# Attention and SwiGLU on one core: the second chunk's preparation moved among the first chunk's products, the down weights' sums stored ahead in DRAM, gated blocks in halves

## The chip, the cores and the metric

One core of one Trainium2 chip (trn2). The metric is the device time of one execution, in microseconds. The kernel before took 1845.11 us (median of three runs, 1843.49 to 1845.51).

## The reference

One layer on two token groups, 1024 and 512 tokens of width 1024, all in float32:

```python
y = neighbourhood_attention(rms_norm(x, norm_mix), na_w_qkv, na_rpb, na_w_o)
x = x + y
x = x + swiglu(rms_norm(x, norm_ffn), ffn_w_gate, ffn_w_up, ffn_w_down)
return rms_norm(x, norm_final)

def swiglu(x, w_gate, w_up, w_down):          # (1024 x 2816), (1024 x 2816), (2816 x 1024)
    return (silu(x @ w_gate) * (x @ w_up)) @ w_down
```

The attention is over windows of 8 rows and 16 columns of a grid 64 wide, 16 heads. The change touches what comes behind it.

## The kernel before

Every float32 operand of a product is split into a high and a low part (`split`, L138 a cast on ScalarE, L139 a subtraction on VectorE), and every product runs in three passes (high by high, high by low, low by high).

The stages follow each other: norm and V projection (to 157 us), attention with its q and k projections (to about 760), the o-projection (L586, its last matmul ends at 803.1), then the feed-forward part and the final norm. x1, the input plus the attention, is kept in DRAM (`x1_d`).

The feed-forward part works on two chunks of 768 tokens. All its big products use a scheme of seven products for a 2x2 block product, with operands that are sums and differences of the four blocks:

- `norm2` and `pair` (L661 to L687) load two x1 tiles, take root and gain (`rms`, L115 to L122), transpose them (L668), and `operands` makes the seven operands: for chunk 0 they are split into `hops` in SBUF, for chunk 1 they are stored to `hop_d` in DRAM. Both happen before the first product of chunk 0, interleaved with the o-projection of the last tiles.
- `unit(c, p, hops)`, 11 for each chunk, does 7 gate and 7 up products (`blocks`, `product`), each of 12 matmuls of 128x384 (L754). The weights come in raw tiles of 512 KB (`w_raw`, L714), `w_ops` makes sums (`wt`) and splits (`wa`, `ws`). ScalarE copies the banks into `c` tiles and applies Silu, VectorE adds and multiplies, and GpSimd makes four sums of gated blocks (`gs`, L800 to L803) and stores seven blocks to `gop_d` (L805).
- Between the chunks the operands of chunk 1 are read back from `hop_d` (L815) and split.
- Down: seven products n, each over 6 token tiles and 11 blocks i; `d_op` loads weight blocks (`dr`, L834) and for four of the seven makes differences on GpSimd (L848 to L857, `tk`), `g_op` loads a whole gated block (`gr`, 128x1408, L864) and splits it into `go`. 33 matmuls of 128x512 (L910) fill a bank. The results are added up in `u2`, `u4` and the `c` tiles, and `finish` (L884 to L893) applies the final norm.

The program is written in this order, and the framework's list scheduler orders the instructions of each engine by its own estimate of their times; on the chip each engine, and each of the three DMA queues (SP's, ScalarE's, GpSimd's), then takes its rows strictly in that order. Buffers come from pools; a pool opened after another is closed takes its space.

## Time and profile before

| | us |
|---|---|
| median of 3 runs | 1845.11 (1843.49 to 1845.51) |
| the profiled execution | 1845.18 |
| its span, first to last instruction | 1843.4 |
| TensorE busy | 1754.1 (95%) |
| VectorE / ScalarE / GpSimd busy | 1192.9 / 863.7 / 448.4 |
| mean granted TensorE clock | 0.985 |
| chunk 0's first product starts | 810.10 |
| chunk 1's first product ends its wait | 1172.54 |
| last up product ends, first down matmul | 1481.6, 1498.72 |
| last addition behind the last down matmul | 1835.16 |

PE is TensorE's matmul, PEld its weight load, DVE VectorE, ACT ScalarE, POOL GpSimd, SP the engine whose queue issues most DMAs; SPq, ACTq and POOLq are the queues. A group's row reads: line, engine, operation, written tile <- read tiles, shape, count | busy us, mean ns of one | idle time before them and what ended it. A row of the timeline reads: start us, length us, then the same, and in brackets the wait before it and what ended it.

### The profile page before, as it was taken

What the parts mean: (1) busy time and instruction counts of PE and PEld (TensorE: products, weight loads), DVE (VectorE), ACT (ScalarE), POOL (GpSimd) and SP (SyncE); (2) the same over time, 40 slices, a digit from 0 to 9 for tenths busy, and PEclk for the clock granted to TensorE, in tenths of its full rate; (3) what the DMA queues carried; (4) which work ended last, traced back from release to release, by engine and by line L of the source; (5) the groups of instructions that cost most, each with busy time, mean ns of one, the idle gap of its engine ahead of it and who ended that gap; (6) DMA issues with size and microseconds to landing.
All of it is one profiled execution on the core that took longest, in us unless ns stands there. A gap on an engine that the chain in (4) does not pass through costs nothing.

```text
span 1843.4 us, 25648 instructions
## 1 busy us (share of the span) xinstructions
PE 1754.1 (95%) x9178; PEld 1522.5 (83%) x9178; DVE 1192.9 (65%) x2191; ACT 863.7 (47%) x1706; POOL 448.4 (24%) x495
## 2 busy tenths in 40 slices
PE   8999999999999999979999999999999969999898
PEld 6877777777767777868999999899999958887676
DVE  4401877777896566768777777867777444545654
ACT  4411776766785554544443444444443333333322
POOL 1211000000130000112243342424243323526420
PEclk9999999999999999988999999999999979999999
DMA  7755334333464443676343434544333277635732
GB/s 245 221 183 160 111 105 113 108 101 103 126 208 146 133 149 100 221 247 185 108 121 118 133 110 151 164 129 125 108 120 107 68 272 245 225 130 191 232 129 100
DMA packets 222048, 278.80 MB, mean 151 GB/s; under 512 B 25600, under 2 KB 171776, under 8 KB 221920
## 3 DMA queue, kind: packets, MB, share of 16 engines
q1 hardware_dynamic: 201824, 210.69, 37.3%
q0 software_dynamic: 18368, 60.18, 9.5%
q10 hardware_dynamic: 1728, 6.29, 1.1%
q8 instruction: 72, 1.18, 0.3%
q14 instruction: 56, 0.46, 0.1%
HBM read 213.20 MB, written 76.43 MB: 157 GB/s over the span
## 4 chain that ended last, share of the span: by engine, by line
PE 68%; DVE 10%; DMA 9%; ACT 5%; issue 3%; SPq 2%; POOL 2%; DVEq 0%; ACTq 0%; POOLq 0%
PE pa L754 20%; PE pd L910 12%; PE pd L754 10%; PE pgv L278 7%; PE pg L332 6%; PE pb L754 5%; DMA vr<-v_d 5%; PE pgo L586 3%; DMA dr<-ffn_w_down 2%; PE pss L394 2%; PE ptt L420 2%; DVE pT L424 2%; SPq L378 2%; PE po L431 2%; ACT s L405 1%
## 5 line engine op out<-in xcount | busy, mean ns | idle before, releaser
L910 PE MATMUL pd<-wd,go 128*128 128x512 f32 x1386 | 323.0, 395 | 30.5 <-ACT go L138 20.4
L910 PEld LDWEIGHTS pd<-wd,go 128*128 128x128 f32 x1386 | 263.0, 191 | 90.4 <-ACT go L138 21.6
L754 PE MATMUL pa<-h,ws 128*128 128x384 f32 x1056 | 201.8, 339 | 2.9 <-ACT c L777 2.1
L754 PE MATMUL pa<-h,wa 128*128 128x384 f32 x1056 | 195.1, 338 | 7.0 <-ACT wa L138 4.5
L754 PE MATMUL pd<-h,ws 128*128 128x384 f32 x1056 | 198.3, 335 | 1.2 <-ACT h L138 0.6
L332 PE MATMUL pg<-hTp,whl 128*128 128x512 f32 x768 | 193.7, 399 | 0.0
L754 PEld LDWEIGHTS pa<-h,wa 128*128 128x128 f32 x1056 | 185.8, 190 | 8.9 <-ACT wa L138 5.2
L139 DVE TENSOR_TENSOR ws<-wt,ws 128x1024 fp32r<-128x1024 f32 x88 | 108.6, 1235 | 127.1 <-ACT ws L138 126.7
L754 PEld LDWEIGHTS pa<-h,ws 128*128 128x128 f32 x1056 | 185.1, 189 | 6.7 <-ACT c L777 4.3
L754 PEld LDWEIGHTS pd<-h,ws 128*128 128x128 f32 x1056 | 184.5, 188 | 1.8 <-ACT h L138 1.0
L332 PEld LDWEIGHTS pg<-hTp,whl 128*128 128x128 f32 x768 | 139.9, 188 | 27.5 <-issue 0.4
L805 POOL DMA_DIRECT2D gop_d<-c x66 | 50.5, 765 | 387.4 <-DVE c L796 380.3
L405 ACT ACTIVATE s<-s,mx 128x384 f32<-128x384 f32 (+1 forms) x192 | 110.7, 580 | 67.3 <-DVE mx L402 67.1
L586 PE MATMUL pgo<-wo,oh 128*128 128x512 f32 x576 | 139.3, 392 | 0.2 <-DVE oh L139 0.2
L139 DVE TENSOR_TENSOR wa<-wr,wa 128x512 fp32r<-128x512 f32 x132 | 117.8, 897 | 18.4 <-ACT wa L138 17.8
L138 ACT CAST ws<-wt 128x1024 fp32r<-128x1024 f32 x88 | 92.6, 1053 | 68.6 <-PE pd L754 65.4
L586 PEld LDWEIGHTS pgo<-wo,oh 128*128 128x128 f32 x576 | 105.6, 188 | 20.7 <-DVE oh L139 0.6
L138 ACT CAST go<-gr 128x1408 fp32r<-128x1408 f32 x42 | 57.7, 1374 | 131.2 <-PE pd L910 114.0
L138 ACT CAST wa<-wr 128x512 fp32r<-128x512 f32 x132 | 81.4, 621 | 62.8 <-PE pb L754 40.0
L754 PE MATMUL pb<-h,wa 128*128 128x384 f32 x528 | 102.0, 340 | 3.4 <-DVE c L774 3.4
L332 PE MATMUL pg<-hTs,whl 128*128 128x512 f32 x384 | 102.6, 404 | 0.8 <-DVE q L343 0.8
L424 DVE TENSOR_TENSOR pT<-ptt,pT 128x384 fp32r<-128x384 f32 (+1 forms) x192 | 90.0, 507 | 17.3 <-ACT pT L423 16.5
(138 smaller groups left out, 2859.6 us busy)
## 6 DMA issues: line engine op xcount, KB each, us to landing
gr<-gop_d SPq DMA_DIRECT2D x42, 704.0 KB
dr<-ffn_w_down SPq DMA_DIRECT2D x99, 256.0 KB
wr<-ffn_w_gate SPq DMA_DIRECT2D x44, 512.0 KB
wr<-ffn_w_up SPq DMA_DIRECT2D x44, 512.0 KB
wr<-na_w_qkv SPq DMA_DIRECT2D x38, 512.0 KB
gop_d<-gs POOLq DMA_DIRECT2D x88, 192.0 KB, 4.4
gop_d<-c POOLq DMA_DIRECT2D x66, 192.0 KB, 2.8
vr<-v_d SPq DMA_DIRECT2D x192, 64.0 KB
```

The source lines that it names most:

```text
L138: nc.scalar.copy(hi, raw)
L139: nc.vector.tensor_tensor(lo, raw, f32(hi), ALU.subtract)
L278: nc.tensor.matmul(pg, hh[a][:, k, c:c + P], wv[k // 2][b][:, k % 2], start=(k == 0 and i == 0), stop=(k == KB - 1 and i == 2))
L332: nc.tensor.matmul(pg, w[:, a, k, :], h[b][:, k, c:c + 512], start=(k == 0 and i == 0), stop=(k == KB - 1 and i == 2))
L378: nc.sync.dma_start(out=raw[:, j * P:(j + 1) * P], in_=src[:, BS[j]:BS[j] + 32, :])
L394: nc.tensor.matmul(pt[:, :n], q[h * HD:(h + 1) * HD, a, j].rearrange("p r i -> p (r i)"), kv[:, krow:krow + nrow, BS[j]:BS[j] + 32], start ...
L405: nc.scalar.activation(s[:, :n], s[:, :n], AF.Exp, bias=mx, scale=-1.0, accum_out=sm)
L424: nc.vector.tensor_tensor(pT[:, :n, 1], pv, f32(pT[:, :n, 0]), ALU.subtract)
L586: nc.tensor.matmul(pg, ohs[k // 4][:, a, k % 4], wo[:, b, k, n * 512:(n + 1) * 512], start=(k == 0 and i == 0), stop=(k == KB - 1 and i == 2))
L754: nc.tensor.matmul(bank[:, :HT], a(y, k), b[:, z, k], start=start and k == 0 and i == 0, stop=k == KB // 2 - 1 and i == 2, skip_group_chec ...
L805: nc.gpsimd.dma_start(out=gop_d[i, 3 * c:3 * c + 3, :, p].rearrange("j q t -> q j t"), in_=a.rearrange("q (j t) -> q j t", j=3))
L910: nc.tensor.matmul(pd, go[:, y, i], wds[i][:, z], start=(i == 0 and m == 0), stop=(i == NP - 1 and m == 2))
```

## The change

Four things, in the order in which they run.

1. The preparation of chunk 1 (`pair1`) becomes a generator, stepped by a `tick` behind each product of units 1, 2 and 3 of chunk 0. It uses four tiles t0 to t3 that exist once each. The gain is applied behind the transposes on VectorE, from a column form `gT` that is loaded at the very start; the root is applied by `nc.scalar.mul`; the operands' differences are made on GpSimd. For chunk 0 `pair0` does the same ahead of the products as before.
2. At the changes (the last unit of chunk 0, the first and last of chunk 1) the up products are interleaved with the gate products at a lag of three, and the operands of chunk 1 are read back (`reload`) one by one behind the last up products of unit (0, 10), through t0 to t3.
3. In chunk 1 `down_sums` makes the differences of down weights that `d_op` made in the down stage, on GpSimd, in 11 iterations, and stores them to DRAM (`wt_d`). It uses t0, t1 and t2.
4. The down stage loads half gated blocks (6 and 5 of the 11) and stored sums, with buffers placed one by one in the space that the last units leave. x1 tiles and half of the results go through GpSimd's queue. The squares and, for the second half of the rows, one multiplication by the final gain are done earlier.

To make room, the weight tiles `wa`, `ws` and `wt` have 2 buffers each (6, 3 and 3 before), with a second pool of 2 for the last `wa` of a block.

```diff
+        gT = cpool.tile([P, KB], F32, name="gT")
+        nc.sync.dma_start(out=gT, in_=g_ffn.rearrange("(k p) -> p k", p=P))
...
+        def pair1(j):
+            xs = []
+            for n, t in enumerate((CT + j, CT + 3 + j)):
+                xn = temp(2 * n)
+                xt = temp(2 * n + 1).rearrange("p (k t) -> p k t", k=KB)
+                yield from norm2(t, xn, xt)
+                xs.append(xt)
+            tt = [temp(2 * n).rearrange("p (s k t) -> p s k t", s=2, k=KB // 2) for n in range(2)]
+
+            def dst(i, op):
+                nc.sync.dma_start(out=hop_d[i, :, :, j * P:(j + 1) * P], in_=op)
+            yield from operands(dst, *xs, [tt[n // 2][:, n % 2] for n in range(4)], nc.gpsimd)
+
+        def down_sums():
+
+            for i in range(NP):
+                x, y, z = temp(0), temp(1), temp(2)
+                nc.sync.dma_start(out=x, in_=w_d[2 * i * P:(2 * i + 1) * P, :])
+                nc.sync.dma_start(out=y, in_=w_d[(2 * i + 1) * P:(2 * i + 2) * P, :])
+                yield
+                b11, b12, b21, b22 = x[:, :512], x[:, 512:], y[:, :512], y[:, 512:]
+                t1, t3 = z[:, :512], z[:, 512:]
+                nc.gpsimd.tensor_tensor(t1, b12, b11, ALU.subtract)
+                yield
+                nc.gpsimd.tensor_tensor(t3, b22, b12, ALU.subtract)
+                nc.gpsimd.dma_start(out=wt_d[0][i * P:(i + 1) * P, :], in_=z)
+                yield
+                nc.gpsimd.tensor_tensor(b11, b22, t1, ALU.subtract)
+                yield
+                nc.gpsimd.tensor_tensor(b12, b21, b11, ALU.subtract)
+                nc.gpsimd.dma_start(out=wt_d[1][i * P:(i + 1) * P, :], in_=x)
+                yield
...
+            order = [0] * 7 + [1] * 7
+            if after:
+                order = [0] * LAG + [x for _ in range(7 - LAG) for x in (1, 0)] + [1] * LAG
...
+        prep = (x for j in range(3) for x in pair1(j))
+        tick = ticks(prep, 1)
+        for p in range(NP - 1):
+            unit(0, p, hops, tick if p else idle)
+            if p == NP - 2:
+                reload(0)
+        unit(0, NP - 1, hops, idle, lambda n: reload(n) if n < 7 else None)
+        sums = down_sums()
+        tick = ticks(sums, 2)
+        for p in range(NP):
+            unit(1, p, hops2, tick if p else idle, None if 0 < p < NP - 1 else lambda n: None)
+        for _ in sums:
+            pass
...
+        SRC = {0: (w_d, 0, 0), 1: (w_d, 1, 0), 2: (w_d, 1, 1), 4: (wt_d[0], None, 0), 6: (wt_d[0], None, 1),
+               5: (wt_d[1], None, 0), 3: (wt_d[1], None, 1)}
...
+        for q in range(84):
+            m, tt, h = q // 12, q % 12 // 2, q % 2
+            n = SEQ[m]
+            g_load(q + 3)
+            g_split(q + 2)
+            if q % 12 < NP:
+                d_load(m + 1, q % 12)
+            if q % 12:
+                d_split(m + 1, q % 12 - 1)
```

Where the instructions stand is set by the scheduler. Three places follow; in the rows, a number behind a tile's name is that of one buffer's use, and the brackets hold the semaphores that a row waits for.

SP's queue in chunk 1, around the raw weights of unit 5. Before (wr_13603 and wr_13605 are the two raw tiles of unit 5's up weights):

```order
L714 DMA wr_13339<-ffn_w_up 128x4x256 [waits DMAHW6_49,DVE_49]
L714 DMA wr_13477<-ffn_w_gate 128x4x256 [waits DMAHW7_49,DVE_49]
L714 DMA wr_13479<-ffn_w_gate 128x4x256 [waits DMAHW0_49,DVE_49]
L714 DMA wr_13603<-ffn_w_up 128x4x256 [waits DMAHW1_49,DVE_49]
L714 DMA wr_13605<-ffn_w_up 128x4x256 [waits DMAHW2_49,DVE_49]
L714 DMA wr_13743<-ffn_w_gate 128x4x256 [waits DMAHW3_49,DVE_49]
```

After (wr_13691 and wr_13693 are those two; t0 and t1 are the loads of the weights' sums, t0_14485 that of the eleventh iteration):

```order
L748 DMA t0_14070<-ffn_w_down 128x1024 [waits DMAHW2_49,DMASW5_49]
L749 DMA t1_14294<-ffn_w_down 128x1024 [waits DMAHW7_49,DMAHW3_49,Pool_49]
L769 DMA wr_13559<-ffn_w_gate 128x4x256 [waits DVE_49]
L748 DMA t0_14293<-ffn_w_down 128x1024 [waits DMAHW6_49,DMAHW1_49,DMASW7_49]
L769 DMA wr_13691<-ffn_w_up 128x4x256 [waits DVE_49]
L749 DMA t1_14486<-ffn_w_down 128x1024 [waits DMAHW7_49,Pool_49]
L748 DMA t0_14485<-ffn_w_down 128x1024 [waits DMAHW4_49,DMAHW1_49,DMASW2_49]
L769 DMA wr_13693<-ffn_w_up 128x4x256 [waits DMAHW5_49,DVE_49]
```

Between the raw weights now stand loads of t0, each with a wait for a DMA of GpSimd's queue (DMASW), and all eleven iterations' loads stand ahead of wr_13693.

GpSimd in chunk 1, around the sums and stores of one unit's gated blocks. Before:

```order
L805 DMA gop_d_81<-c_12760 128x3x128 [waits DMASW0_49,DVE_49]
L800 TENSOR_TENSOR gs_12930<-c_12746,c_12760 128x384 [waits DVE_49]
L801 TENSOR_TENSOR gs_12931<-gs_12930,c_12719 128x384 [waits Pool_49]
L802 TENSOR_TENSOR gs_12932<-c_12719,c_12746 128x384
L803 TENSOR_TENSOR gs_12933<-c_12803,gs_12931 128x384 [waits DVE_49,Pool_49]
L805 DMA gop_d_81<-c_12803 128x3x128 [waits DMASW1_49]
L805 DMA gop_d_81<-gs_12933 128x3x128 [waits DMASW2_49,Pool_49]
L805 DMA gop_d_81<-gs_12930 128x3x128 [waits DMASW3_49]
```

After (t2_12888 and t0_12886 belong to the third iteration of the weights' sums, gs_12415 to gs_12418 to unit (1, 0)):

```order
L753 TENSOR_TENSOR t2_12888<-t0_12886 128x512 [waits DMAHW7_49,DMASW4_49]
L755 TENSOR_TENSOR t2_12888<-t1_12887,t0_12886 128x512 [waits DMAHW5_49]
L758 TENSOR_TENSOR t0_12886<-t1_12887,t2_12888 128x512 [waits DMASW5_49,Pool_49]
L876 TENSOR_TENSOR gs_12415<-c_12231,c_12287 128x384 [waits DVE_49]
L756 DMA wt_d0_81<-t2_12888 128x1024 [waits DMASW7_49,Pool_49]
L877 TENSOR_TENSOR gs_12416<-gs_12415,c_12204 128x384 [waits Pool_49]
L878 TENSOR_TENSOR gs_12417<-c_12204,c_12231 128x384
L879 TENSOR_TENSOR gs_12418<-c_12371,gs_12416 128x384 [waits DVE_49,Pool_49]
L881 DMA gop_d_83<-c_12371 128x3x128 [waits DMASW0_49]
L881 DMA gop_d_83<-gs_12418 128x3x128 [waits Pool_49]
L881 DMA gop_d_83<-gs_12415 128x3x128
L881 DMA gop_d_83<-gs_12416 128x3x128 [waits DMASW3_49]
```

The unit's gated sums, which stood alone, now stand inside an iteration of the weights' sums, between its third and its fourth subtraction.

ScalarE in chunk 0, at the first gate products of a unit: of unit 2 after, of one of the first units before. Before:

```order
L792 ACTIVATE c_9464<-c_9464 128x384 [waits DVE_49]
L777 COPY c_9491<-pa_9449 128x384 [waits PE_49]
L780 COPY c_9505<-pd_9451 128x384 [waits PE_49]
L138 CAST ws_9569<-wt_9566 128x1024 [waits Activation_49]
L792 ACTIVATE c_9505<-c_9505 128x384 [waits DVE_49]
```

After (t1 and t3 take the squares of two x1 tiles, L675 scales them; c_9633 and c_9669 are the unit's first two copies of pa):

```order
L669 ACTIVATE t1_9636,ms_9651<-t0_9635 128x1024 [waits DMAHW3_49]
L669 ACTIVATE t3_9725,ms_9744<-t2_9724 128x1024 [waits DMAHW7_49,DMAHW4_49,DVE_49]
L827 COPY c_9633<-pa_9618 128x384 [waits PE_49]
L141 CAST wa_9754<-wr_9750 128x512 [waits Activation_49]
L141 CAST wa_9772<-wr_9752 128x512
L141 CAST wa_9757<-wr_9752 128x512 [waits PE_49,Activation_49]
L675 ACTIVATE t0_9635<-t0_9635,rs_9655 128x1024 [waits Activation_49,Pool_49]
L866 ACTIVATE c_9633<-c_9633 128x384 [waits DVE_49]
L675 ACTIVATE t2_9724<-t2_9724,rs_9748 128x1024 [waits Activation_49,Pool_49]
L834 COPY c_9669<-pa_9618 128x384 [waits PE_49]
L838 COPY c_9684<-pd_9620 128x384 [waits DMASW5_49,PE_49]
```

The Squares and scalings of chunk 1's tiles now stand between the copies and casts of the unit, where only these stood.

389 lines of the change are left out of this document (233 added, 156 removed).

## The prediction

> **What bounds the kernel now.** I read the share of each engine first, then the stage windows, then the places where TensorE stands still. The columns of the windows are: stretch, length, busy time and count of TensorE, weight load, VectorE, ScalarE and GpSimd, granted clock, DMA share, GB/s.
>
> ```profile
> PE 1754.1 (95%) x9178; PEld 1522.5 (83%) x9178; DVE 1192.9 (65%) x2191; ACT 863.7 (47%) x1706; POOL 448.4 (24%) x495
> PEclk9999999999999999988999999999999979999999
> ...
> 806.00:816.00 10.00, 3.34 (x9) 2.60 (x9) 5.03 (x9) 3.16 (x6) 0.87 (x1) 0.63 1.03 342
> 847.00:1150.00 303.00, 303.00 (x1733) 300.98 (x1732) 225.68 (x296) 129.50 (x214) 106.46 (x111) 1.00 0.41 124
> 1150.00:1180.00 30.00, 25.56 (x142) 24.09 (x141) 27.05 (x35) 17.50 (x27) 10.02 (x10) 1.00 0.64 210
> 1180.00:1475.00 295.00, 295.00 (x1697) 293.64 (x1696) 205.20 (x270) 118.38 (x195) 105.72 (x111) 1.00 0.36 109
> 1475.00:1502.00 27.00, 9.45 (x45) 8.12 (x44) 12.78 (x18) 9.88 (x14) 8.41 (x10) 0.67 0.71 248
> ```
>
> TensorE bounds it. Inside the two chunks of up and gate products it never stops (303.00 of 303, 295.00 of 295), while GpSimd has two thirds of its time free. What is to be had lies at three seams: the start of chunk 0, the change of chunk, the start of down. Inside down there is one more:
>
> ```profile
> 803.10 1.04 PE L668 MATMUL pt<-ident,xn 128*128 128x128 f32 x8
> 810.10 3.34 PE L754 MATMUL pa<-h,wa 128*128 128x384 f32 x9 [4.53 <-ACT wa L138]
> 1152.28 4.17 PE pa L754 x24
> 1163.34 7.30 DMA hr<-hop_d
> 1479.36 2.24 PE L754 MATMUL pa<-h,wa 128*128 128x384 f32 x12
> 1498.72 1.22 PE L910 MATMUL pd<-wd,go 128*128 128x512 f32 x2 [17.12 <-ACT go L138]
> 1510.00:1590.00 80.00, 80.00 (x355) 66.24 (x354) 1.00 0.77 266
> 1690.00:1765.00 75.00, 62.83 (x255) 48.87 (x254) 0.95 0.68 223
> 1835.16 0.69 DVE L896 TENSOR_TENSOR u<-u,pd 128x512 f32<-128x512 f32 x1 [3.03 <-PE pd L910]
> ```
>
> A product of 12 matmuls takes 4.17 / 2 = 2.085 us, a unit of 14 products 29.2. The o-projection ends at 803.1, the last up product at 1481.6: 678.5 us against 22 × 29.2 + 48 transposes at 1.04 / 8 = 648.6. So 29.9 are lost, 30 − 25.56 = 4.4 of them at the change of chunk and 25.5 at the start. Down takes 1835.1 − 1481.6 = 353.5; its 1386 matmuls at 80.00 / 355 = 0.2254 need 312.4. Lost: 41.1, of which 17.1 before its first matmul, 12.2 idle in 1690 to 1765, the rest at a lower clock around these (0.67 in 1475 to 1502).
>
> **The change, part by part.** The sum is made against the profiled run's 1845.2 (1843.4 of span and 1.8 around it), 0.1 above the median.
>
> *Load of gT first on SP's queue.* 1024 elements of 4 bytes ahead of the first x tile. No row has its like; a whole 512 KB load is the nearest:
>
> ```profile
> 1010.60 4.64 SPq L714 DMA_DIRECT2D wr<-ffn_w_gate  x2
> ...
> 1013.50:1014.00 0.50, 0.50 (x4) 0.50 (x4) 0.50 (x1) 0.00 (x0) 0.50 (x1) 1.00 0.47 164
> 1014.00:1014.50 0.50, 0.50 (x5) 0.50 (x4) 0.50 (x1) 0.00 (x0) 0.50 (x2) 1.00 0.02 8
> ```
>
> Issued at 1010.6, its bytes are through by about 1014.1: 3.5. The price of gT lies between nothing and that; I take +1.5, nearer to nothing, since it moves 4 KB.
>
> *Start of chunk 0.*
>
> ```profile
> L138 ACT CAST wa<-wr 128x512 fp32r<-128x512 f32 x132 | 81.4, 621 | 62.8 <-PE pb L754 40.0
> L139 DVE TENSOR_TENSOR ws<-wt,ws 128x1024 fp32r<-128x1024 f32 x88 | 108.6, 1235 | 127.1 <-ACT ws L138 126.7
> L138 ACT CAST ws<-wt 128x1024 fp32r<-128x1024 f32 x88 | 92.6, 1053 | 68.6 <-PE pd L754 65.4
> L741 DVE TENSOR_TENSOR wt<-wr x17: 683/684/686, 902.6 to 1136.6; 128x512 f32<-128x512 f32 x17
> ```
>
> The last chunk-1 preparation (hop stores, six loads, splits) leaves it. The first raw tile and its cast now stand ahead of the o-projection's end, so the first product follows at once. The second raw tile lies where wo lay and is loaded from 803.1 on: 3.5 to land and a cast of 0.62, so the second product starts at about 807.3. For the third, ws needs VectorE's two sums (0.7 each, beside subtractions of wa), a Square of 1.06 ahead of it on ScalarE, a cast of 1.05 and a subtraction of 1.24: about 812. Some 4 to 5 are lost, and 2 to 3 to the lower clock (0.63 there before): 7 (5 to 12) instead of 25.5, −18.5.
>
> *Units 2 and 3 of chunk 0.* The scaling of x1 (L675) needs the root from GpSimd, which stands behind the gated sums of the unit before. Behind the scaling, on ScalarE, stands the copy of pa for which the fifth product waits.
>
> ```profile
> 888.90 4.32 PE L754 MATMUL pa<-h,wa 128*128 128x384 f32 x24
> 892.02 1.00 POOL L800 TENSOR_TENSOR gs<-c 128x384 f32<-128x384 f32 x1 [1.81 <-DVE c L796]
> ...
> 898.01 3.06 POOL L805 DMA_DIRECT2D gop_d<-gs  x4
> L119 POOL TENSOR_TENSOR rs<-me,mhalf 128x1 f32<-128x1 f32 x24 | 14.3, 597 | 75.5 <-DVE me L117 75.4
> L115 ACT ACTIVATE xt<-xn 128x1024 f32<-128x1024 f32 x12 | 12.7, 1060 | 14.7 <-DMA xn<-x_d 6.5 <-issue 2.4 <-DVE h L139 2.4
> 1015.33 0.53 ACT L792 ACTIVATE c<-c 128x384 f32<-128x384 f32 x1 [2.39 <-DVE c L774]
> 1015.77 0.46 ACT L777 COPY c<-pa 128x384 f32<-128x384 f32 x1
> ```
>
> A unit begins at 891.0 (the second product from 888.90); GpSimd is free at 901.1, 10.1 later. Two roots of 0.60, two scalings like the Square's 1.06, a Silu and the copy, half a microsecond each: 14.4 after the unit's start, where the fifth product is due at 4 × 2.085 = 8.3. Waiting 6.1, twice: +12 (7 to 15, since the reload of t0 can be later too; less if the order lets the root go first).
>
> *Change of chunk.* The lagged products give the reload three units' room: 4.4 to about 2, −2.4.
>
> *The weights' sums in chunk 1.* Per iteration: load of t0, four subtractions of 128x512 on GpSimd, store of t0. There is one t0, so the next load waits until the store has landed, and these loads stand on SP's queue ahead of the weights: the one of the eleventh iteration ahead of the second raw tile of unit 5's up weights. Whatever the serial cycle costs, the weights wait for it.
>
> ```profile
> L802 POOL TENSOR_TENSOR gs<-c 128x384 f32<-128x384 f32 x22 | 31.6, 1437 | 0.0
> L848 POOL TENSOR_TENSOR tk<-dr,tk 128x512 f32<-128x512 f32 x11 | 19.7, 1811 | 12.4 <-DMA dr<-ffn_w_down 12.4
> L851 POOL TENSOR_TENSOR tk<-dr 128x512 f32<-128x512 f32 x11 | 17.6, 1613 | 9.4 <-DMA dr<-ffn_w_down 9.4
> L915 POOL TENSOR_TENSOR c<-c,u 128x512 f32<-128x512 f32 x6 | 7.8, 1293 | 52.8 <-ACT u L914 52.8
> gop_d<-gs POOLq DMA_DIRECT2D x88, 192.0 KB, 4.4
> v_d<-vs POOLq DMA_DIRECT2D x24, 256.0 KB, 3.4
> o_d<-oT POOLq DMA_DIRECT2D x24, 256.0 KB, 2.6
> es_d<-t_d POOLq DMA_DIRECT2D x8, 768.0 KB, 5.2
> ```
>
> Load: 3.5. Subtractions: 1.29 undisturbed, 1.81 at worst; beside this VectorE even 384 elements take 1.44, so I take 1.7, four are 6.8. Issue of the store 3.06 / 4 = 0.76. Landing between 2.6 to 3.4 (256 KB) and 5.2 (768 KB, which also reads DRAM): 3.6. Cycle 14.7. Counted from unit (1,0): GpSimd is done with unit (0,10) at about 11, the first store has landed at 22; nine more cycles are 132; the gated sums of units 0 and 2 stand inside the third and the eighth iteration (10 each), those of unit 1 cost about 3 behind the fifth. The last load goes out at 177, the weights behind it land at 181, their cast and the copy queued behind it end at 182. TensorE wants that copy for the third product of unit 5, at 5 × 29.2 + 4.2 = 150. Loss 32, and 2 for the lower clock after waits: +34. Nothing gives it back: when the sums are done the units run at 29.2 again. With 1.29 and a landing of 2.6 the cycle is 12.1 and the loss about 6; with 1.81 and 5.2 it is 16.7 and the loss 52.
>
> By the Trainium skill, page "DMA: Bandwidth & Descriptors", section "Anatomy of one DMA", a transfer costs about 2.0 us plus its bytes over 436 GB/s; an estimate from this is 3.2 for 512 KB. The load's 3.5 agrees nearly; with 3.2 for load and store the cycle would be 14.0 and the sum 6 lower.
>
> *Down.*
>
> ```profile
> L139 DVE TENSOR_TENSOR wd<-tk,wd 128x512 fp32r<-128x512 f32 x33 | 32.2, 1018 | 7.5 <-ACT wd L138 6.9
> ```
>
> The blocks of tiles 0 to 2 were stored in chunk 0, and their loads now wait for single buffers of the last units, not for the closing of the pools; the first tile is then paced by 11 splits of 1.02 against 33 × 0.2254: 11.2 − 7.4 = 3.8. The sums on GpSimd, which shared buffers dr with the loads, are gone from 1690 to 1765, and half blocks with three buffers are split ahead. 41.1 becomes about 7 (4 and 3): −34. Bounds: −25, if only the idle 29.3 goes and 4 come back, to −37.
>
> *Tail.*
>
> ```profile
> 1836.56 0.61 ACT L884 ACTIVATE yo<-c 128x512 f32<-128x512 f32 x1
> ```
>
> The second half is squared and scaled by gf before the last sum, and its last scaling moves to ScalarE beside VectorE's: this Square with its read of the sum (0.19) and about as much again, −1.4 (0 to −2).
>
> *Costed at nothing.* Transposes move in among the products of chunk 0 (48 either way). The gain applied on VectorE behind the transposes, and the scaling on ScalarE, lie for chunk 0's tiles under the o-projection, where TensorE does not wait; without that cover 1.06 a tile. Weight buffers shrink from 6 and 3 to 2: still a block ahead, and the first late cast would cost its 1.7 to 2.3. The sums add 11 MB of loads and 11 of stores to chunk 1, 75 GB/s to its 109; the DMA share 0.36 leaves room. In down, x tiles and the first half's results go through GpSimd's queue at 0.76 an issue, where the subtractions of 1.29 to 1.81 were.
>
> Sum: 1.5 − 18.5 + 12 − 2.4 + 34 − 34 − 1.4 = −8.8. 1845.2 − 8.8 = 1836.4, so 1836.
>
> **Rivals.**
> - *The sums are hidden.* Subtractions at 1.29, quick stores, cycle 12.1 or less: the loss is 6 or nothing. For it: GpSimd idles 190 of 295 us in chunk 1. Against it: VectorE's 205.20 of 295 and 1.44 for 384 elements. 1836 − 28 = 1808.
> - *The cycle is dearer, and the kernel slower.* Place: store of t0 to load of t0 on SP, ahead of the weights. Each microsecond more per cycle is nine; above 16.1 the time passes 1848.8 (14.7 + 12.4 / 9). At 16.7: 1836 + 18 = 1854. For it: gop_d stores from GpSimd's queue take 4.4 for only 192 KB. Against it: those queue four deep. A second way to the same end: the stores are late because GpSimd writes their descriptors beside a busy VectorE. From the rows, 4.4 for 192 KB and (5.2 − 2.6) / 512 per KB for 320 more make 6.0, 2.4 above what I took: 1836 + 9 × 2.4 = 1858. Against it: the issues take an even 0.76. The Trainium skill, page "SBUF — State Buffer", section "SBUF: two separate sides", states this mechanism for VectorE operations that hold the port shared with GpSimd; the even 0.76 does not bear it out here.
> - *Down does not start earlier.* If its first loads still wait for the end of the units, 13 of the 34 stay: 1849. Against it: only chunk 1's blocks are late, and they are used from the fourth tile.
>
> **Chances.** Cycle of 13 to 16.1 as worked out: 0.55, within it 1821 to 1849. Sums hidden: 0.17. Dearer cycle: 0.20, of it 0.06 by late descriptors. Down late: 0.08. 0.2% is 3.7 us, about what a measurement of this kernel can tell from no change. The first case, whose other terms move it by some 10 as well, gives faster 0.33, same 0.12, slower 0.10; the second is faster; the third slower 0.16, same 0.04; the fourth slower 0.06, same 0.02. Together faster 0.50, same 0.18, slower 0.32. The range reaches from the hidden sums (1808, 1 below it) to the dear cycle with one more wait of 9, 1863.
>
> **What would show it.** TensorE waits in chunk 1, spread over units 3 to 5 and none after, put down to ScalarE's wa and behind it to loads of t0 or of wr; iterations 14 to 15 us apart; two waits of 6 early in chunk 0; at most 4 us before down's first matmul and none above 1 later. Wrong if chunk 1 shows no waits (then near 1808), or if waits in chunk 0 or down add up to more than 25.

## The result and the profile after

The changed kernel takes 1871.4 us (median; 1869.85 to 1872.34) against 1845.2 for the kernel before on the same chip: ratio 1.0143, interval 1.0126 to 1.0161. It is slower by 26 us where 9 us of gain were forecast, and lies 8 us above the range. Its profiled execution took 1872.3, with a span of 1870.6.

The page, first, and the stretches that answer to those of before (same columns):

```profile
PE 1770.9 (95%) x9178; PEld 1533.8 (82%) x9178; DVE 1212.4 (65%) x2229; ACT 874.8 (47%) x1742; POOL 495.0 (26%) x569
...
PEclk9999999999999999999999999988889999999999
```

```profile
803.00:1120.00 317.00, 306.18 (x1732) 302.78 (x1732) 230.68 (x311) 139.54 (x226) 119.02 (x121) 0.98 0.49 151
1120.00:1155.00 35.00, 31.77 (x170) 30.81 (x170) 32.14 (x34) 20.61 (x32) 17.97 (x15) 0.95 0.61 193
1155.00:1385.00 230.00, 187.81 (x990) 183.92 (x990) 155.64 (x167) 69.87 (x118) 137.56 (x132) 0.90 0.56 190
1385.00:1530.00 145.00, 144.91 (x832) 144.29 (x831) 100.58 (x131) 58.96 (x97) 52.40 (x55) 1.00 0.33 104
1230.00:1245.00 15.00, 6.19 (x26) 5.87 (x25) 7.58 (x7) 2.82 (x6) 5.86 (x6) 0.67 0.59 189
...
1690.00:1765.00 75.00, 75.00 (x324) 60.53 (x324) 44.46 (x58) 25.13 (x40) 34.86 (x36) 1.00 0.60 188
```

The shares on the page hardly differ from before. The stretches do: from 1155 to 1385, where the weights' sums run, TensorE is busy 187.81 of 230 at a granted clock of 0.90; from 1385 on, with the sums done, it is full again (144.91 of 145). Where it stands, in TensorE's timeline (start, length, in brackets the wait before it):

```profile
808.88 1.01 PE L809 MATMUL pb<-h,wa 128*128 128x384 f32 x2 [4.32 <-ACT wa L141]
...
876.92 3.85 PE L809 MATMUL pa<-h,ws 128*128 128x384 f32 x12 [2.23 <-ACT c L827]
...
913.08 3.21 PE L809 MATMUL pa<-h,ws 128*128 128x384 f32 x12 [2.67 <-ACT c L827]
...
1149.83 3.92 PE L809 MATMUL pa<-h,wa 128*128 128x384 f32 x12 [2.77 <-DVE c L841]
...
1241.11 4.21 PE L809 MATMUL pa<-h,ws 128*128 128x384 f32 x12 [8.81 <-ACT c L827]
...
1270.08 4.21 PE L809 MATMUL pa<-h,ws 128*128 128x384 f32 x12 [5.70 <-ACT c L834]
1304.09 4.21 PE L809 MATMUL pa<-h,ws 128*128 128x384 f32 x12 [5.85 <-ACT c L827]
1331.38 4.21 PE L809 MATMUL pa<-h,ws 128*128 128x384 f32 x12 [9.38 <-ACT c L827]
...
1364.06 4.21 PE L809 MATMUL pa<-h,ws 128*128 128x384 f32 x12 [8.90 <-ACT c L834]
...
1537.49 0.96 PE L1051 MATMUL pd<-wd,go 128*128 128x512 f32 x3 [2.31 <-DVE wd L142]
...
1548.74 314.90 PE L1051 MATMUL pd<-wd,go 128*128 128x512 f32 x1352 [0.23 <-DVE wd L142]
```

Five waits of 5.7 to 9.4 lie in chunk 1 (with the short ones 42.1 in all), and the product behind each of them takes 4.21 us instead of 2.24. The granted clock is 0.67 over 1230 to 1245, wait and product together, and 0.50 while the product runs (1241 to 1245). Down has short waits at its start only (4.4 in all); from 1548.74 its last 1352 matmuls run without a stop, 314.90 / 1352 = 0.2329 each.

Taken apart by the starts of the units' first products (a loss is what a stretch takes beyond 29.2 a unit):

| step | forecast, change of time | measured |
|---|---|---|
| until the o-projection's end | +1.5 | −0.8 (802.3, was 803.1) |
| start of chunk 0 | −18.5 | −15.2 (loss 7.9; was 23.1, without its 6.2 of transposes) |
| units 1 to 4 of chunk 0 | +12 | +10.1 (31.0 + 35.7 + 35.7 + 30.7, less 4 × 29.2 and 6.2 of transposes) |
| change of chunk | −2.4 | +0.3 (5.6 + 0.5; was 5.8) |
| chunk 1, the weights' sums | +34 | +58.5 |
| down, from the last up product to the last matmul | −34 | −23.9 (329.6; was 353.5) |
| tail | −1.4 | −1.3 |
| sum | −8.8 | +27.7 (spans: +27.2; the units of before took 29.25, not 29.2) |

### The profile page after: what moved, and what is told of

It reads as the page before. It is cut to its first block, busy times and chain, and to the rows that moved or that the text cites. A ratio compares the mean times of both kernels' runs of the same rounds, so it can differ in the third digit from the quotient of the medians.

```text
span 1870.6 us, 25937 instructions
## 1 busy us (share of the span) xinstructions
PE 1770.9 (95%) x9178; PEld 1533.8 (82%) x9178; DVE 1212.4 (65%) x2229; ACT 874.8 (47%) x1742; POOL 495.0 (26%) x569
## 4 chain that ended last, share of the span: by engine, by line
PE 34%; DMA 7%; POOL 5%; issue 3%; DVE 3%; ACT 0%; SPq 0%; POOLq 0%; ACTq 0%; DVEq 0%
PE pd L1051 15%; PE pa L809 11%; PE pd L809 5%; PE pb L809 3%; DMA wt_d<-t 3%; DMA t<-ffn_w_down 2%; DMA gr<-gop_d 1%; POOL gop_d L881 1%; POOL t L758 1%; DVE wa L142 1%; POOL t L760 1%; DMA dr<-ffn_w_down 1%; DMA hop_d<-t 0%; POOL gs L879 0%; DMA gop_d<-gs 0%
## 5 line engine op out<-in xcount | busy, mean ns | idle before, releaser
L809 PE MATMUL pa<-h,ws 128*128 128x384 f32 x1056 | 211.8, 351 | 45.5 <-ACT c L827 30.1
L809 PEld LDWEIGHTS pa<-h,ws 128*128 128x128 f32 x1056 | 193.7, 198 | 50.5 <-ACT c L827 32.3
L809 PEld LDWEIGHTS pd<-h,ws 128*128 128x128 f32 x1056 | 189.2, 192 | 0.0
L142 DVE TENSOR_TENSOR ws<-wt,ws 128x1024 fp32r<-128x1024 f32 x88 | 116.8, 1328 | 106.2 <-ACT ws L141 106.1
L809 PE MATMUL pa<-h,wa 128*128 128x384 f32 x792 | 149.4, 341 | 6.2 <-DVE c L841 6.1
L809 PEld LDWEIGHTS pa<-h,wa 128*128 128x128 f32 x792 | 140.9, 190 | 8.6 <-DVE c L841 8.0
L142 DVE TENSOR_TENSOR wa<-wr,wa 128x512 fp32r<-128x512 f32 x132 | 129.6, 997 | 16.0 <-ACT wa L141 14.8
L141 ACT CAST go<-gr 128x768 fp32r<-128x768 f32 x84 | 65.6, 781 | 155.4 <-PE pd L1051 112.0
L142 DVE TENSOR_TENSOR go<-gr,go 128x768 fp32r<-128x768 f32 x84 | 82.6, 986 | 73.4 <-ACT go L141 71.9
```

Of the source, the lines that this page charges most:

```text
L141: nc.scalar.copy(hi, raw)
L142: nc.vector.tensor_tensor(lo, raw, f32(hi), ALU.subtract)
L809: nc.tensor.matmul(bank[:, :HT], a(y, k), b[:, z, k], start=start and k == 0 and i == 0, stop=k == KB // 2 - 1 and i == 2, skip_group_chec ...
```

## Experiments

"Loss of chunk 1" is the time from its first product to its last less 11 × 29.2 = 321.2: 59.0 in the changed kernel. Diffs are against the changed kernel unless another run is named.

**What the sums cost in all.** No sums at all; down takes plain rows of the weights in their place.

```diff
-        sums = down_sums()
+        sums = iter(())
...
-        SRC = {0: (w_d, 0, 0), 1: (w_d, 1, 0), 2: (w_d, 1, 1), 4: (wt_d[0], None, 0), 6: (wt_d[0], None, 1),
-               5: (wt_d[1], None, 0), 3: (wt_d[1], None, 1)}
+        SRC = {0: (w_d, 0, 0), 1: (w_d, 1, 0), 2: (w_d, 1, 1), 4: (w_d, None, 0), 6: (w_d, None, 1),
+               5: (w_d, None, 0), 3: (w_d, None, 1)}
```

> The sums of down weights are left out: no loads, subtractions or stores in chunk 1, and the down stage loads raw rows of the down weights of the same size in their place (so its results are not the reference's). Both theories: chunk 1 runs at 29.2 to 29.4 us a unit behind its first one, 57 us less, time about 1814. Rival (the smaller weight buffers or the lagged units slow chunk 1): units still above 31, time above 1835.

1812.4 us (ratio to before 0.982); chunk 1 loses 1.4, each of units 0 to 9 takes 29.3. The sums are the whole loss of chunk 1, and everything else in the change together gains 33 us.

**SP's queue.** First, the loads of t0 and t1 on GpSimd's queue, so that SP carries only weights:

```diff
-                nc.sync.dma_start(out=x, in_=w_d[2 * i * P:(2 * i + 1) * P, :])
-                nc.sync.dma_start(out=y, in_=w_d[(2 * i + 1) * P:(2 * i + 2) * P, :])
+                nc.gpsimd.dma_start(out=x, in_=w_d[2 * i * P:(2 * i + 1) * P, :])
+                nc.gpsimd.dma_start(out=y, in_=w_d[(2 * i + 1) * P:(2 * i + 2) * P, :])
```

> The loads of the weights' sums (t0, t1) go through GpSimd's queue instead of SP's; the serial cycle of load, sums and store stays. Queue theory (weights wait on SP behind a load that waits for a store): the waits of TensorE in chunk 1 (42 us, and some 15 us at the lower clock behind them) vanish but for what GpSimd's longer queue holds back in gated blocks; units of chunk 1 at 29.3 to 31 us, time 1815 to 1830. Rival (the sums themselves are too dear: they slow VectorE and the DMAs, and the products wait for those): the units stay at 38 to 52 us in the middle of the chunk, time above 1860.

1841.2 (0.9978, 0.9963 to 0.9994), loss 34.1. The 25 us that are gone speak for the queue, but the time lies above the 1815 to 1830 expected of it, and a new wait of 14 has come. ScalarE's timeline, about 1334 us:

```profile
1334.80 0.48 ACT L838 COPY c<-pd 128x384 f32<-128x384 f32 x1 [16.29 <-POOL gs L876]
```

The copy needs a `c` buffer that GpSimd's gated sums free, and these now stand behind loads on GpSimd's own queue. The other way leaves the loads on SP and holds SP to the order in which the program is written:

```diff
-        for p in range(NP):
-            unit(1, p, hops2, tick if p else idle, None if 0 < p < NP - 1 else lambda n: None)
-        for _ in sums:
-            pass
+        with in_order(nc.sync):
+            for p in range(NP):
+                unit(1, p, hops2, tick if p else idle, None if 0 < p < NP - 1 else lambda n: None)
+            for _ in sums:
+                pass
```

> SP's queue in chunk 1 keeps the order in which the program is written: the eleven pairs of sum loads stand 2 to 4 weight loads apart, the last ahead of unit 8's up weights instead of unit 5's; loads, sums and stores are the same. Queue theory: an iteration has 20.9 us where the serial cycle takes 16.5 to 25, so the weights are never late; units 29.3 to 29.8, chunk 1 about 55 us shorter, time 1813 to 1822. Rival (sums too dear by themselves): the units stay slow, spread over more of the chunk, time above 1850.

1838.6 (0.9953, 0.9933 to 0.9973), loss 25.2, above the 1813 to 1822 expected. The place of the loads ahead of the weights is worth 34 of the 59 us; 25 are left that the queue does not explain, which neither theory had.

**What the other 25 are.** The same with GpSimd's four subtractions replaced by memsets of the same tiles (four lines like this one); GpSimd then writes as before, in 0.53 us each, but reads nothing:

```diff
-                nc.gpsimd.tensor_tensor(t1, b12, b11, ALU.subtract)
+                nc.gpsimd.memset(t1, 0.5)
```

> Beside e5 (SP in program order): each of the 44 subtractions on GpSimd becomes a memset of the same 128x512 tile, which reads no SBUF; loads, stores, queues and their order stay (the down stage then multiplies constants, so the results are not the reference's). In e5 five units of chunk 1 still took 32 to 35 us. Contention theory (VectorE's subtractions take 1.3 to 2.3 us instead of 0.69 while GpSimd's subtractions read SBUF, and the casts and additions behind them come late): those units fall to 29.3 to 30, chunk 1 some 20 us shorter than e5's, time 1815 to 1822. Order theory (GpSimd takes its rows in order, stands waiting for t0, and hands the gated blocks' c tiles back late): the units stay at 32 to 35, time 1833 to 1840.

1814.9 (0.9844, 0.9814 to 0.9873), loss 3.4. Length of VectorE's subtraction for wa in 1185 to 1380 (shortest, median, longest in ns), in program order with subtractions and then with memsets:

```profile
L142 DVE TENSOR_TENSOR wa<-wr,wa x36: 677/1073/3278, 1193.0 to 1372.1; 128x512 fp32r<-128x512 f32 x36
```

```profile
L142 DVE TENSOR_TENSOR wa<-wr,wa x41: 677/692/1869, 1185.4 to 1379.6; 128x512 fp32r<-128x512 f32 x41
```

VectorE is slower beside GpSimd's subtractions and not beside its memsets: in 1160 to 1480 of the run with memsets, the 7 such operations that overlap with a memset and with no GpSimd arithmetic take 0.687 us in the mean. (The long ones left there, to 1.869, stand beside the gated sums.) The two timelines of the changed kernel show it row by row (VectorE, then GpSimd):

```profile
1239.15 1.22 DVE L142 TENSOR_TENSOR ws<-wt,ws 128x1024 fp32r<-128x1024 f32 x1
1240.40 1.64 DVE L800 TENSOR_TENSOR wt<-wr 128x512 f32<-128x512 f32 x1
1241.97 1.76 DVE L801 TENSOR_TENSOR wt<-wr,wt 128x512 f32<-128x512 f32 x1
```

```profile
1229.76 0.57 POOL L761 DMA_DIRECT2D wt_d<-t  x1 [0.30 <-POOL t L760]
...
1240.23 1.26 POOL L753 TENSOR_TENSOR t<-t 128x512 f32<-128x512 f32 x1 [9.14 <-DMA t<-ffn_w_down]
1241.47 1.72 POOL L755 TENSOR_TENSOR t<-t,t 128x512 f32<-128x512 f32 x1
1243.14 1.72 POOL L758 TENSOR_TENSOR t<-t,t 128x512 f32<-128x512 f32 x1
```

What takes 0.69 alone takes 1.64 and 1.76 here, in step with GpSimd's rows. The Trainium skill, page "SBUF — State Buffer", section "SBUF: two separate sides", says that a VectorE operation with two SBUF inputs and a GpSimd operation that reads SBUF take one port pair in turns, each for its whole length. These rows and the memsets agree.

The trace of before had it too, at the gated sums (VectorE, then GpSimd):

```profile
1215.37 0.69 DVE L741 TENSOR_TENSOR wt<-wr 128x512 f32<-128x512 f32 x1
...
1220.87 1.50 DVE L745 TENSOR_TENSOR wt<-wr 128x512 f32<-128x512 f32 x1
1222.29 1.50 DVE L746 TENSOR_TENSOR wt<-wr,wt 128x512 f32<-128x512 f32 x1
```

```profile
1220.47 1.35 POOL L801 TENSOR_TENSOR gs<-gs,c 128x384 f32<-128x384 f32 x1
1221.78 1.47 POOL L802 TENSOR_TENSOR gs<-c 128x384 f32<-128x384 f32 x1
```

The memsets also shorten each iteration, so this run's time alone does not separate GpSimd's subtractions from the pace; a later run does. First came the obvious remedy, the subtractions on VectorE (program order kept; all four lines like this one):

```diff
-                nc.gpsimd.tensor_tensor(t1, b12, b11, ALU.subtract)
+                nc.vector.tensor_tensor(t1, b12, b11, ALU.subtract)
```

> Beside e5: the 44 subtractions are done on VectorE instead of GpSimd. Contention theory: 44 x 0.69 = 30 us more on VectorE, but its other operations go back to their length beside an idle GpSimd; VectorE has 321 - 205 = 116 us free in chunk 1; units 29.3 to 30, time 1814 to 1822. Rival (VectorE is the engine that is short, whoever does the sums): units 30.5 to 33, time above 1830.

1835.9 (0.9956, 0.9942 to 0.9969), loss 27.0: missed. The wait for the loads has moved to VectorE, whose splits stand behind it:

```profile
DVE t L753 <- DMA t<-ffn_w_down: 34.4, 7, 6.0
```

Two runs built on this one missed as well. The first leaves the sums as they are and aims at units 2 to 4 of chunk 0: four empty steps behind each pair of tiles (`for _ in range(4): yield` at the end of `pair1`), together with the address shift that is explained below:

> e7, and ident 128 bytes wider (as e4), and four empty steps behind each pair of chunk 1's preparation, so that a pair's x1 loads come some 8 us after the last difference of the pair before. Expected on top of e7: down 8 us less from the addresses; units 2 to 4 of chunk 0, which lost 10.9 us to Squares that wait for reloaded t0 and t2 and to roots behind the gated sums, lose 2 to 6; together 12 to 17 less than e7, time 1799 to 1806. If the units of chunk 0 lose 10.9 as before, the spacing was not what they lacked: 1807 to 1812.

1836.2 (0.9957, 0.9939 to 0.9974): chunk 1 loses 22.8, and in chunk 0 units 3 and 4 now take 37.9 and 35.6 (35.4 and 30.7 in the run before it). The empty steps moved the waits on and removed none. The second holds each subtraction behind the VectorE row that was written last before it (diff against the run with the sums on VectorE):

```diff
-                nc.vector.tensor_tensor(t1, b12, b11, ALU.subtract)
+                behind(nc.vector, lambda: nc.vector.tensor_tensor(t1, b12, b11, ALU.subtract))
```

> Beside e7 (sums on VectorE, SP in program order) each subtraction must stand, in VectorE's order, behind the last VectorE row that is written before it, the additions of that step's product. In e7 VectorE stood 34 us in the first subtraction (L753) waiting for the load of t0, and chunk 1 still lost 27 us. If that wait was the loss: VectorE's wait for t0 falls under 5 us, units 29.3 to 30, chunk 1 loses 2 to 8, time 1814 to 1821. If VectorE is simply short in chunk 1: units stay 30 to 34, time above 1830.

1866.9 (1.0111, 1.009 to 1.0131), loss 54.4. The subtractions come later, so t0 is free later, and SP again holds the weights behind its load:

```profile
SPq L757 <- DMA wt_d<-t: 258.1, 10, 42.0
```

**Own buffers for the results.** The sums go to t2 and t3, so that t0 and t1 only take loads, and each load is issued behind the last subtraction that reads its tile, four products ahead of its use. Down's addresses and the reload are as in the two sections behind this one.

```diff
+            def load(i):
+                x, y = temp(0), temp(1)
...
+                (x, y), z, v = new, temp(2), temp(3)
...
+                minus(z[:, :512], b12, b11)
                 yield
...
+                minus(z[:, 512:], b22, b12)
...
+                minus(v[:, :512], b22, z[:, :512])
                 yield
...
+                minus(v[:, 512:], b21, v[:, :512])
+                nc.gpsimd.dma_start(out=wt_d[1][i * P:(i + 1) * P, :], in_=v)
+                if i + 1 < NP:
+                    new = load(i + 1)
```

With `minus` on GpSimd:

> The same buffers and loads, with the subtractions on GpSimd as in the changed kernel. In the run with memsets in their place chunk 1 lost 3.4 us, which has two readings. If the subtractions slow VectorE by reading SBUF beside it, some 20 us of loss stay (25 in the run with SP in program order): 1871.4 - 8 - 4 - 39 = 1820, between 1817 and 1827. Rival: the memsets helped because each iteration came to its store sooner; then with t0 free of the store the loss falls below 8: 1802 to 1809.

1836.6 (six runs from 1826.9 to 1839.0; 0.995, 0.9934 to 0.9966), above the 1817 to 1827 expected of slower VectorE rows and far above the rival's 1802 to 1809. The loss is 26.9 in the profile, which is of the shortest of the six. SP waits for GpSimd 0.6 us in all of chunk 1, no weight is late for want of a load, and the loss is still there with VectorE's long subtractions:

```profile
SPq L757 <- POOL gs L899: 0.4, 1, 0.4
```

```profile
L151 DVE TENSOR_TENSOR wa<-wr,wa x36: 676/1244/3285, 1189.0 to 1369.0; 128x512 fp32r<-128x512 f32 x36
```

Paired by time in 1160 to 1480, the 30 of these that have no GpSimd arithmetic beside them take 0.683 us in the mean, the 24 that overlap with some in part 1.96, and the 7 that lie wholly beside it 1.58. So it is GpSimd's subtractions beside VectorE, not the pace of the iterations. With `minus` on VectorE, held by `behind` as above:

> The run before it (sums on VectorE, aligned operands, reload on VectorE) with the four results in t2 and t3, so that t0 and t1 hold loads only and the next load waits for the last subtraction instead of a landed store; each load is issued directly behind that subtraction, four products ahead of its use. If the wait that held the chunk was the load of t0 behind its own store, with the weights queued behind it, chunk 1 loses 8 us or less (54 in the run with the store), and of the changed kernel's 1871.4 go 51 to 57 there, 8 by the addresses and 4 at the change of chunk: 1802 to 1809. Rival: VectorE has no room for 44 subtractions at these places and the splits come late whatever the buffers: chunk 1 loses 20 or more, 1820 and above.

1867.9 (1.0119, 1.0105 to 1.0134), loss 68.8: missed by far. Freed of the store, t0 now waits for the subtraction itself:

```profile
SPq L757 <- DVE t L762: 183.8, 10, 33.6
```

By the order of the program, the row that was written last before a subtraction is often a split of the block that is being prepared, and that split needs weights which SP holds behind the load of t0: a circle, if this reading is right. Without `behind`, the scheduler places the subtractions:

> The run with sums on VectorE and own buffers, without the dependency that holds each subtraction behind the row of VectorE written last: in that run SP stood 184 us for t0, 34 at the longest, because the subtraction that frees t0 stood behind splits of weights that SP holds behind the same t0. The scheduler now places the subtractions among the additions of the same products. If the circle was the cause, chunk 1 loses 8 us or less (26.9 with GpSimd's subtractions, 68.8 with the circle): 1826.9 of the profiled run with GpSimd's subtractions less 19 or more: 1802 to 1808. VectorE would then wait under 5 us for t<-ffn_w_down (34.4 in the first run with sums on VectorE). Rival: 44 subtractions of 0.7 to 0.8 us more on VectorE, 205 of 295 us busy before, are themselves too much between the splits, on whichever engine they read SBUF: the loss stays at 20 to 27 and the time at 1820 to 1830.

1842.2 (0.9988, 0.9979 to 0.9997), loss 41.0: missed too, above both the 1802 to 1808 and the rival's 1820 to 1830. The circle is gone (SP waits 2.4 for t1 and not at all for t0) and the splits are short again (wa's median 692), but VectorE stands for loads and stores of t:

```profile
DVE t L762 <- DMA t<-ffn_w_down: 32.7, 7, 6.2
...
DVE t L762 <- DMA wt_d<-t: 16.5, 2, 8.3
```

Last, each subtraction behind the last addition of a product (these follow TensorE's pace, and nothing on SP), and SP without the program order, so that single loads of t0 and t1 stand between raw weights (diff against the run before this):

```diff
+        def add(o, a, b):
+            nc.vector.tensor_tensor(o, a, b, ALU.add)
+            added[0] = next(k for k in reversed(nc.cur_bb.bb.instructions) if k.engine == nc.vector.engine)
...
-            a = next(k for k in reversed(traced) if k.engine == eng.engine)
+            a = added[0]
...
-                nc.vector.tensor_tensor(o, a, b, ALU.subtract)
+                behind(nc.vector, lambda: nc.vector.tensor_tensor(o, a, b, ALU.subtract))
...
-        with in_order(nc.sync):
```

> The same sums on VectorE with own buffers; each subtraction stands behind the addition of the last product ahead of it (so that TensorE sets its pace, two products apart, and its load, issued four products earlier, has landed), and SP's queue is left to the scheduler, which now puts single loads of t0 and t1 between raw weights. In the run before it (41.0 lost in chunk 1) the splits ran at their old lengths again (wa 904 ns against 1274), but VectorE stood 32.7 us for t<-ffn_w_down and 16.5 for stores. If only these waits were left, chunk 1 loses 8 or less and the time is 1803 to 1809. Rival: any order in which one queue carries both the sums' loads and the weights makes one wait for the other: 20 or more stay, 1815 to 1835.

**1808.6 us (1806.0 to 1810.3); ratio to before 0.9794, 0.9778 to 0.9809.** Chunk 1 loses 7.2. This version beats both kernels, the changed one by 62.8: 51.8 in chunk 1, 8.6 in down, 5.2 at the change of chunk, less 2.5 until the o-projection's end. It differs from the run before it in two things, the place of the subtractions and SP's order; no run separates them. Its chunk 1, as a stretch, its splits, and the longest waits of TensorE and SP:

```profile
1185.00:1380.00 195.00, 192.15 (x1100) 190.23 (x1099) 161.89 (x220) 79.34 (x133) 78.23 (x90) 1.00 0.66 215
```

```profile
L157 DVE TENSOR_TENSOR wa<-wr,wa x41: 677/683/1503, 1184.8 to 1379.0; 128x512 fp32r<-128x512 f32 x41
```

```profile
PE pa L835 <- ACT c L860: 4.2, 8, 0.7
```

```profile
SPq L763 <- DVE t L768: 44.0, 10, 8.2
```

VectorE is busy 161.89 of 195, more than before (145.86 there), and TensorE does not mind; SP still waits 44 us for t0, but no wait of TensorE in chunk 1 is longer than 0.8.

**Addresses of operands in down.** The 33 matmuls of a bank ran at 227 ns a matmul before and at 233 after, at the same clock:

```profile
1510.00:1530.00 20.00, 20.00 (x90) 16.57 (x89) 8.49 (x9) 8.55 (x12) 3.88 (x3) 1.00 0.87 296
```

```profile
1600.00:1620.00 20.00, 20.00 (x88) 16.08 (x87) 7.42 (x9) 6.24 (x12) 0.00 (x0) 1.00 0.45 139
```

The addresses of moving and stationary operand in the built program agree modulo 256 bytes before, and differ by 128 after for 1170 of the 1386 matmuls. The other 216 tell the two apart within one run: behind them the next matmul follows at 227 ns as before (mean 228.4), behind the 1170 at 233.2. Sixteen columns became forty-eight in a tile at the start, which shifts what is allocated behind it on that side by 128 bytes:

```diff
-        ident = cpool.tile([P, P + 16], F32, name="ident")[:, :P]
+        ident = cpool.tile([P, P + 48], F32, name="ident")[:, :P]
```

> One number: the constant tile ident is 128 bytes a partition wider, so all tiles on the left side of SBUF lie 128 bytes higher. In both traces a matmul takes 227 ns (128x512) where its two operands' addresses agree modulo 256 and 232 to 233 where they differ by 128; down has 19 of its 22 weight buffers on the left and its gated blocks on the right, at different remainders. Address theory: down's matmuls go from 233 to 227 ns, down 8 us shorter; attention's q and k products gain up to 2, the V projection changes by 0 to 3 either way; time 1871 - 8 = 1863 (1860 to 1867). Rival (half blocks cost the matmuls: more semaphores, smaller tiles): 233 ns stays, time 1871 within 2.

1863.7 (1.010, 1.0083 to 1.0118): down takes 319.6 from its first to its last matmul (328.7), 227 ns each again; the V projection, which the change had brought from 233 to 229 in the mean, goes back to 232.5, and the o-projection ends 2.9 later. Met.

**The change of chunk.** With that shift and the sums as in the run "behind the row written last", all subtractions of the reload on VectorE:

```diff
-                (nc.gpsimd if n in (2, 4) else nc.vector).tensor_tensor(lo, r, f32(hi), ALU.subtract)
+                nc.vector.tensor_tensor(lo, r, f32(hi), ALU.subtract)
```

> e10, ident 128 bytes wider (as e4), and all subtractions of the reload at the change of chunk on VectorE (two of seven operands' were on GpSimd). Down 8 to 9 us shorter by the addresses. The last unit of chunk 0 and the first of chunk 1 lost 4 to 6 us together, with VectorE busy without a pause: if GpSimd's subtractions slowed VectorE there more than they took off it, the loss falls to 1 to 3; if VectorE is short there, it grows by 1 to 3. Time 1804 to 1811 by the first, 1809 to 1816 by the second.

1859.3 (1.0067, 1.0043 to 1.0091), far above the 1804 to 1816 expected, since the run that it builds on had missed by some 50. At the change of chunk, the last unit of chunk 0 and the first of chunk 1 take 29.6 + 30.5, in the run that it builds on 33.2 + 29.3, in the changed kernel 34.8 + 29.7: 1.7 lost instead of 4.1 and 6.1. With fewer operations on GpSimd, VectorE, which now does more, holds TensorE up less.

**Units 1 to 4 of chunk 0.** On the run before this one, Squares and scalings are held behind ScalarE's last written row, the Squares two steps later and the scalings one more (the scaling's lines):

```diff
-            nc.scalar.mul(xn, xn, rs)
+            yield
+            behind(nc.scalar, lambda: nc.scalar.mul(xn, xn, rs))
```

> e11, and in chunk 1's preparation the Square stands three steps behind its load and the scaling two behind the Square, each behind the ScalarE rows written before it. Units 2 to 4 of chunk 0 lost 10.9 us: ScalarE waited 0.9 to 1.4 for each load, some 2 for each root, with the copies of pa behind. If the order on ScalarE did that, they lose 2 to 5 and the time is 6 to 9 below e11's, 1797 to 1804; if the roots are late wherever they stand, 8 to 11 as before.

1874.1 (1.0147, 1.0124 to 1.0169): missed, and 15 slower than the run that it builds on. Units 1 to 5 take 30.2, 36.9, 37.9, 32.2 and 41.2, and one wait is now 7.03:

```profile
1008.61 4.21 PE L822 MATMUL pa<-h,ws 128*128 128x384 f32 x12 [7.03 <-ACT c L840]
```

## Why the prediction was wrong, and where it held

**The weights' sums: the step that failed.** The mechanism was named: one t0, its load behind its store, the weights on SP behind that load. Putting the queue in another order gives back 34 of 59 us. Two waits of the changed kernel show it, SP's for t1 and t0:

```profile
SPq L749 <- POOL t L760: 101.8, 10, 17.3
SPq L748 <- DMA wt_d<-t: 60.6, 10, 11.1
```

One such load of t0, in SP's timeline, between the store at 1229.76 and the subtraction at 1240.23 shown above:

```profile
1235.70 0.33 SPq L748 DMA_DIRECT2D t<-ffn_w_down  x1
```

The term was mis-sized in three ways.
- The cycle is 16.0 to 17.1 where no gated sums stand in it, not 14.7. From that load at 1235.70 to the first subtraction at 1240.23 are 4.5 (3.5 forecast), from the issue of the store at 1229.76 to that load 5.9 (4.4); the subtractions, 1.26 to 1.72, were as forecast. That is the rival "the cycle is dearer", which had 0.20 and 1854 to 1858. The prediction's other price, 3.2, goes by the Trainium skill, page "DMA: Bandwidth & Descriptors", section "Anatomy of one DMA", which gives its figures for DMAs that GpSimd issues. The load is SP's, and the 4.5 here lies further from 3.2 than from 3.5.
- The waits come to 42 where 32 were forecast, and the lower clock behind them to some 17, not 2: each of the five long ones makes the next product 4.21 instead of 2.24, at a granted clock of 0.50 (1241 to 1245), and some of the products after that take 3.2.
- VectorE was taken to be free for what it had to do. The sum priced what VectorE does to GpSimd ("beside this VectorE even 384 elements take 1.44") and left out the other direction, although the trace of before holds it. With SP in program order this is 22 of the remaining 25 us (25.2 with subtractions, 3.4 with memsets). The prediction named the right place of the Trainium skill, page "SBUF — State Buffer", section "SBUF: two separate sides", and used it for descriptors only. The stores' issues take an even 0.57, so no row shows late descriptors; what makes the way from a store to the next load 1.5 longer than forecast stays open.

The three overlap, since a wait of 42 us in all holds what the slower VectorE adds to it. The range missed because its dear end was the price of the cycle and one more wait of 9, with 2 us for the clock and nothing for VectorE.

**Down: right in mechanism, too large by 10.** 7 us were to be left over the pure matmuls, 17.2 were. Some 9 of them are the slower spacing by the operands' addresses, a term that the sum did not have; the shift of 128 bytes gave them back (328.7 to 319.6). The waits at the start of down are 4.4 of them, and some 4 are not taken apart. The stretch from 1690 to 1765, which lost 12.2 before, is full.

**Change of chunk: failed.** A gain of 2.4 was forecast and none came. (The wait that ended at 1172.54 before was that of chunk 1's seventh product; its first began at 1154.20.) The lagged products did spread the reload, but in 1120 to 1155 VectorE is busy 32.14 of 35 and its addition came 2.77 late. Without the weights' sums 4.1 are lost there (33.2 + 29.3), and with the two reload subtractions taken from GpSimd as well 1.7, about the 2 that were forecast: the gain was there, and GpSimd's subtractions beside VectorE took it.

**Start of chunk 0: held.** 7 forecast, 7.9 measured, with one wait of 4.32 for the second raw tile's cast as worked out; the third product did not wait.

**Units of chunk 0: size and units held, the wait was another.** 12 forecast as two waits of 6; measured are 4.4 in each of units 2 and 3 and 1.5 in unit 4. The fifth product was to wait for a copy behind the scaling, which waits for the root. It waits 0.44. The long wait is the third product's, and its copy stands behind two Squares, the first of which waits for its load (ScalarE, about 876; the scaling comes last):

```profile
873.24 1.06 ACT L669 ACTIVATE t<-t 128x1024 f32<-128x1024 f32 x1 [0.86 <-DMA t<-x_d]
...
875.36 1.06 ACT L669 ACTIVATE t<-t 128x1024 f32<-128x1024 f32 x1 [0.96 <-DVE me L671]
...
876.41 0.46 ACT L827 COPY c<-pa 128x384 f32<-128x384 f32 x1
...
880.73 1.16 ACT L675 ACTIVATE t<-t,rs 128x1024 f32<-128x1024 f32 x1 [2.30 <-POOL rs L673]
```

That the sum comes near 12 is in part luck: these waits are 2.2 and 2.7, and slower products behind them make up the rest. Empty steps and later Squares and scalings both made it worse; what would remove these 10 us is open.

**The rivals.** The hidden sums would have been 1808: leaving the sums out gave 1812.4, and the version that hides them, with the addresses mended, 1808.6. A late down fell: its first matmul comes 0.9 behind the last up product.

**Small terms.** The tail's −1.4 was −1.3. gT's +1.5 cannot be seen, since the V projection's gain by its addresses and a scatter between runs (801.0 to 804.0 at the o-projection's end without the shift) cover it; in the eight runs with that gain undone the o-projection ended between 802.8 and 807.7 (803.1 before), so a price of about that size fits but is not shown.

## What to carry to other kernels

Work that is moved to an idle engine is paid twice when it slows a busy one: look in the trace of before for a group whose shortest and longest lengths differ by a factor of two (677 to 1500 ns here), and see what the neighbour does during the long ones. A load that waits for a buffer belongs neither ahead of the bound engine's loads on the same queue nor on an engine whose other rows are urgent. The version that hid the sums gave it its own buffer, and its consumer a place that is paced by the bound engine (behind the additions of a product), not by a queue that it holds up itself. Price a wait of TensorE with the slow products behind it: the 5.7 us at 1270 became 8.6, since the next two products took 4.21 and 3.19 instead of 2.24.

## What the hardware showed that had not been expected

- TensorE's spacing depends on the operands' addresses. 128x512 matmuls with both operands at the same place modulo 256 bytes follow each other at 227 ns, 128 bytes apart at 233, at a granted clock of 1.00. It was seen in down, there even within the one run, and, the other way round, in the V projection; moving the tiles by 128 bytes exchanged the two.
- A VectorE subtraction of 128x512 takes 0.683 us alone and 1.6 to 2.0 in the mean (3.3 at the longest) beside GpSimd's subtractions, while memsets on GpSimd leave it at 0.69.
- After a wait of 5.7 us or more a product of 12 matmuls takes 4.21 us instead of 2.24, at a granted clock of 0.50 (1241 to 1245). The Trainium skill, page "TensorE: Matmul & The Clock Gate", section "Part 1: The HAM clock gate", states half the clock after some 3.4 us without work; the five waits agree with it, but a wait of 2.77 was followed by 3.92, nearly as much, and one of 2.23 by 3.85. So in this trace shorter waits bring the low clock too.
